# A hybrid decoder layer on one core: operands of the first gate/up row moved to VectorE, two weight loads and a statistic moved across a stage boundary

## The chip, the cores and the metric

The kernel runs on one core of a Trainium2 chip. A core has five engines with instruction queues of their own that run in the order written: TensorE (PE in the profile, its weight loads as PEld), VectorE (DVE), ScalarE (ACT), GpSimd (POOL) and SyncE (SP). They meet through semaphores. SP, ACT and POOL also issue DMAs. The metric is the device time of one execution in microseconds (us), as the median of three runs: 1428.53 us, from 1426.43 to 1428.83.

## The reference, cut to what matters

Batch 1, 1024 tokens, width 1024, all float32. Three sub-layers follow each other, each with a norm before and after:

```python
h = hybrid_mixer(rmsnorm(x, norms[l, 0]), ...)      # NSA attention (512) | short conv (512)
x = x + rmsnorm(h, norms[l, 1])
h = memory_attention(rmsnorm(x, norms[l, 2]), rmsnorm(mem, mem_norm[l]), mem_wq, mem_wkv, mem_wo)
x = x + rmsnorm(h, norms[l, 3])
h = swiglu(rmsnorm(x, norms[l, 4]), ffn_wg, ffn_wu, ffn_wd)   # hidden width 2816
x = x + rmsnorm(h, norms[l, 5])
# end of the mixer:
merged = jnp.concatenate([rmsnorm(o_nsa, gn_nsa), rmsnorm(o_conv, gn_conv)], axis=-1)
return merged @ w_out
# swiglu:
return (jax.nn.silu(h @ wg) * (h @ wu)) @ wd
```

## The kernel before, in words

Tokens are cut into eight rows of 128. A matmul operand is split into a high and a low part (`split`: ACT copies the high part at line 119, another engine subtracts for the low part at line 120), and a product is three matmuls, high by high, high by low and low by high (`mm3`, lines 123 to 125). With four blocks of depth a product is 12 matmuls of 512 columns.

The program has stages. **Attention** takes the token rows in order; for each pair of heads it leaves its output in the tile `on` (GpSimd, line 730), which SP stores to DRAM (`on_d`). After the last pair of a row the sum of squares of that row is made for the group norm: ScalarE squares `on` into `sq` (line 799), TensorE adds over partitions with `ones` (line 802), and `rsqrt` (VectorE, ScalarE twice, VectorE) leaves one column of `gn`. The projections of the conv half are filled in between. At its end GpSimd loads the output weights of the attention half (`load_wo`, line 199) and the query weights of the memory attention (`wq`, line 811, two tiles of 1 MB), and then the stage's other constants (line 848).

The **middle stage** holds the output projection, the memory attention and the norms. It is a list of small units in one line of text (`L` load, `M` split, `P` project, `N` norm, `X` transpose, `Q` query, ...). For token row n, `u_load` requests `on` (256 KB), `pt` (512 KB, the conv half) and `x` (512 KB) on SP; `u_merge` splits `on` into `mh` and `ml`; `u_proj` makes 24 matmuls `p<-big,mh`; `u_post` (lines 898 to 908) adds `pt`, normalises, adds to `x`. The tiles `on`, `pt` and `x` have two buffers each, and SP takes the requests in order. Sixteen products of the next stage (`G`, four for each of its rows 1 to 4) fill TensorE's time at the end.

The **gate/up stage** cuts tokens and depth in halves and multiplies 2 by 2 blocks with seven products instead of eight, for gate and for up. It runs over 11 rows j; a row takes the hidden columns of blocks j and j+11. A row needs the eight weight blocks `raw` (256 KB each, `ff_load`), sums and differences of these (`s3`, and in place in `raw`: lines 1184 to 1186 and 1190), splits of them (`ah`, `al`), and the token operands B11, B21, T2, T3, T1, T4, B22. In row 0 the latter five do not stand yet: `build_t` (line 1124) makes the differences of the token blocks and splits them. Row 0 has 14 products, rows 1 to 4 have 10 each. The **down stage** follows.

The order of instructions on each engine comes from a scheduler, which goes by priorities (the order of the code) and by its own estimate of when operands are there; DMAs may be bound to come after an instruction (`tc.issue_after`). So a change in one place moves instructions in others.

Of the kernel before, what the change touches and what calls it, by code (L numbers as in the profile page):

```python
# [66 lines left out]
def hymba_kernel(ctx: ExitStack, tc: tile.TileContext, a, out: bass.AP):  # L67
# [134 lines left out]
    with ExitStack() as st:  # L202
# [363 lines left out]
            load_wo(k)  # L566
        proj_k("s", C_KS)


    ap2 = pool(at_stack, "ap2", bufs=2)  # L570
    with ExitStack() as st:
# [120 lines left out]
        def pv_stage(i, h0, pc, psel, pwin, w0):  # L692
# [32 lines left out]
            if h0 % 4 == 2:  # L725
                tmp = ap2.tile([64, 2, 2, 2, P], F32, name="otmp", bufs=1)
                for x in range(2):
                    A.activation(tmp[:, x], po4[0][64 * x:64 * x + 64], AF.Copy)
                for par in range(2):
                    Gp.tensor_tensor(ons[i][par * 64:(par + 1) * 64, h0 // 2 - 1:h0 // 2 + 1, :],  # L730
                                     tmp[:, 0, :, par, :], tmp[:, 1, :, par, :], OP.add)
            if h0 == H - 2:
                Y.dma_start(on_d[i], ons[i])
# [48 lines left out]
        for n, (i, h0) in enumerate(tasks):  # L782
            ahead = run_soft(n + SKEW)
            pv = pv_stage(i, h0, cmps[i][1], *soft.pop(n))
            steps = next(pv)
            acc = OFF[i]
            for _ in pv:
                acc += RATE[i] / steps
                while acc >= 1:
                    acc -= 1  # L790
                    next(ahead, None)
            for _ in ahead:
                pass
            if n in (9, 21, 29, 30):
                with tc.issue_after(last["norm"].ins):
                    load_wo((9, 21, 29, 30).index(n))
            if h0 == H - 2:
                sq = ap2.tile([P, 4, P], F32, name="sq", bufs=1)
                A.activation(sq, ons[i], AF.Square)
                pn = psf.tile([P, 1], F32, name="f")  # L800
                for c in range(4):
                    T.matmul(pn, sq[:, c, :], ones[:, 0:1], start=c == 0, stop=c == 3)
                V.tensor_copy(gn[:, i:i + 1], rsqrt(small, pn, 512, 1, "gn"))
                for m in range(FILL[n // 4], FILL[n // 4 + 1]):
                    fill(m)
        for m in range(FILL[NT], 2 * NT):
# [1 line left out]
        wq = []  # L808
        for c in range(2):
            wq.append(big_tile().bitcast(F32R).rearrange("p a b -> p (a b)"))  # L810
            Gp.dma_start(wq[c], wq_d[c].rearrange("p x c -> p (x c)"))
            wq[c] = wq[c].rearrange("p (x k c) -> p x k c", x=2, k=KT)
    at_stack.close()

# [16 lines left out]
    def en(k):  # L831
        return V if EN[k] == "V" else Gp
# [39 lines left out]
    def u_merge(n):  # L872
        on = ld[n][0]
        mh = em.tile([P, 4, P], F32R, name="mh", bufs=2)
        ml = em.tile([P, 4, P], F32R, name="ml", bufs=2)
        split(mh, ml, on, en("M"))
        mrg[n] = mh, ml

    def u_proj(n):
        mh, ml = mrg.pop(n)  # L880
# [171 lines left out]
                fload(k)  # L1052

    def ff_raw():
        return ff["s"].tile([P, 4, P], F32, name="raw", bufs=10)

    def ff_load(w, q, j):
        c, k0 = (j + HF if q[0] == "2" else j), (4 if q[1] == "2" else 0)
# [59 lines left out]
    with ExitStack() as st:  # L1118
# [5 lines left out]
        def build_t():  # L1124
            hi = bp.tile([P, 4, 512], F32R, name="T2h")
            lo = bp.tile([P, 4, 512], F32R, name="T2l")
            for k in range(4):
                x0, x1, x2, x3 = a0[:, k, :], b0[:, k, :], a1[:, k, :], b1[:, k, :]
                V.tensor_tensor(x0, x1, x0, OP.subtract)
                tmp = sp1.tile([P, 512], F32, name="tmp")  # L1130
                V.tensor_tensor(tmp, x3, x0, OP.subtract)
                split(hi[:, k, :], lo[:, k, :], tmp, en("T2"))
                Gp.tensor_tensor(x1, x3, x1, OP.subtract)
                Gp.tensor_tensor(x2, x2, tmp, OP.subtract)
            bop["T2"] = hi, lo
            put_b("T3", b0, en("T3"), bp)
            put_b("T1", a0, en("T1"), bp)
            put_b("B22", b1, en("B22"), bp)
            put_b("T4", a1, en("T4"), bp)
# [3 lines left out]

        for j in range(HF):
            t = {}
            s1 = sp1.tile([P, S], F32, name="sg", bufs=3)
            s2 = sp1.tile([P, S], F32, name="sg", bufs=3)
            raw = {(w, q): ff_load(w, q, j) for w in range(2) for q in ("11", "12", "21", "22")}

            def put(w, dst, src0, src1):  # L1150
                if w == 0:
# [17 lines left out]
            for w in range(2):  # L1169
# [2 lines left out]
                    Y.dma_start(c, c1_d[j - 1, w])  # L1172
                    put(w, s1[:, ta], None, c)
                else:
                    put(w, s1[:, ta], prod(raw[w, "12"], "B21", Gp), t[w, 1])
            if j == 0:
                build_t()
                assert tc.cur_priority < after_mid + 3000, (tc.cur_priority, after_mid)
# [2 lines left out]
            for w in range(2):  # L1181
                s3 = late.tile([P, 4, P], F32, name="s3")
                t[w, "s3"] = s3
                Gp.tensor_tensor(s3, raw[w, "11"], raw[w, "21"], OP.subtract)  # L1184
                Gp.tensor_tensor(raw[w, "21"], raw[w, "21"], raw[w, "22"], OP.add)
                Gp.tensor_tensor(raw[w, "11"], raw[w, "21"], raw[w, "11"], OP.subtract)
            for w in range(2):
                m = prod(raw[w, "11"], "T2", V)
                V.tensor_tensor(t[w, 1], t[w, 1], m, OP.add)
                Gp.tensor_tensor(raw[w, "12"], raw[w, "12"], raw[w, "11"], OP.subtract)  # L1190
            for w in range(2):
                m = prod(t[w, "s3"], "T3", V)
                t[w, 3] = late.tile([P, 512], F32, name="t3")
# [230 lines left out]
```

## Time and profile before

| what | value |
|---|---|
| median of three runs | 1428.53 us |
| profiled execution, its own time | 1429.11 us |
| its span, from first to last instruction | 1427.3 us |
| mean granted TensorE clock | 0.974 |
| busy: PE / DVE / ACT / POOL | 1349.8 / 940.2 / 682.6 / 497.2 us |
| attention's last matmul of the main chain | about 567 us |
| middle stage's first projection | 579.85 us |
| gate/up row 0 on PE | 796.6 to 849.6 us |
| gate/up row 1 and later | 849.6 to about 1191 us |
| DMA | 203.28 MB, mean 142 GB/s |

The span is the time between the first and the last instruction; 1.8 us lie around it. A long busy share of PE does not say that PE is the limit everywhere: the profile's slices show two places where PE is idle and its clock is granted at half, near 570 us and near 810 us. There the question is which wait ends last. A "row" of a timeline gives the start, the time from the first start to the last end of the group, and in brackets how long the engine had been idle and what released it.

### The profile page before, as it was taken

The page shows a single profiled execution, that of the slowest core. Times are in us where ns is not written, and L with a number is a line of the kernel's source. Part 1 is how long each engine was busy: PE and PEld are TensorE (multiplying, and loading weights), DVE is VectorE, ACT ScalarE, POOL GpSimd, SP SyncE. Part 2 cuts the span into 40 slices and gives each one's busy share as a digit, 9 for nine tenths or more (in the row PEclk, how much of TensorE's full clock was granted, in tenths as well). Part 3 has the DMA queues.
Part 4 walks back from the last instruction along what each step waited for, and adds up shares of the span by engine and source line. Part 5 has one row for each costly group of instructions (what it writes and reads, how often), then busy time and mean ns, then how long its engine had stood idle before and what let it go on. Part 6 is the DMA issues. An engine that isn't in the chain of part 4 may idle for free.

```text
span 1427.3 us, 19754 instructions
## 1 busy us (share of the span) xinstructions
PE 1349.8 (95%) x6748; PEld 1127.1 (79%) x6748; DVE 940.2 (66%) x2071; ACT 682.6 (48%) x1465; POOL 497.2 (35%) x472
## 2 busy tenths in 40 slices
PE   8999999999999998798779899999999999989997
PEld 6987788888989887677668678888888887867885
DVE  6444553447899995468886786654544444998787
ACT  5433334327878886256675432333333333444463
POOL 1232332227767664111120766654444531000000
PEclk9999999999999999799989899999999999999999
DMA  7587466494733303943246455432222226930213
GB/s 229 146 282 266 142 221 194 151 233 104 149 67 68 75 8 133 351 158 104 91 136 195 125 170 158 144 118 74 89 89 82 82 89 214 375 112 30 67 59 118
DMA packets 161061, 203.28 MB, mean 142 GB/s; under 512 B 8530, under 2 KB 115198, under 8 KB 156703
## 3 DMA queue, kind: packets, MB, share of 16 engines
q1 hardware_dynamic: 128416, 146.44, 32.2%
q0 software_dynamic: 31392, 53.48, 13.5%
q10 hardware_dynamic: 1152, 2.10, 0.4%
q8 instruction: 53, 0.87, 0.3%
q14 instruction: 48, 0.39, 0.1%
HBM read 138.54 MB, written 63.44 MB: 142 GB/s over the span
## 4 chain that ended last, share of the span: by engine, by line
PE 75%; DVE 12%; issue 4%; DMA 4%; ACT 3%; POOL 1%; SPq 0%; DVEq 0%; POOLq 0%; ACTq 0%
PE m L125 13%; PE m L124 13%; PE m L123 13%; PE mm L125 4%; PE mm L123 4%; PE mm L124 4%; PE o L718 3%; PE t L712 2%; DVE ptl L120 1%; PE s L642 1%; PE s L643 1%; DVE psel L659 1%; PE mm L228 1%; PE tr L485 1%; PE p L123 1%
## 5 line engine op out<-in xcount | busy, mean ns | idle before, releaser
L119 ACT ACTIVATE ah<-raw 128x512 fp32r<-128x512 f32 x132 | 83.0, 631 | 212.3 <-PE m L124 188.8
L125 PE MATMUL mm<-hh,wl 128*128 128x512 f32 x320 | 125.5, 394 | 2.2 <-POOL wl L120 2.2
L123 PE MATMUL mm<-hh,wh 128*128 128x512 f32 x320 | 126.6, 396 | 0.1
L124 PE MATMUL mm<-hl,wh 128*128 128x512 f32 x320 | 125.6, 393 | 0.0
L120 DVE TENSOR_TENSOR al<-raw,ah 128x512 fp32r<-128x512 f32 x118 | 107.1, 908 | 24.8 <-ACT ah L119 24.8
L124 PE MATMUL m<-bl,ah 128*128 128x512 f32 x264 | 102.9, 397 | 3.7 <-DVE bl L120 3.7
L125 PE MATMUL m<-bh,al 128*128 128x512 f32 x264 | 102.0, 397 | 2.5 <-DVE al L120 2.5
L120 POOL TENSOR_TENSOR wl<-wr,wh 128x1024 fp32r<-128x1024 f32 x22 | 54.0, 2456 | 134.9 <-ACT wh L119 134.9
L1161 POOL TENSOR_TENSOR sg<-sg,tmp 128x512 f32<-128x512 f32 x44 | 66.0, 1500 | 80.6 <-DVE tmp L1160 36.8
L124 PE MATMUL m<-big,ah 128*128 128x512 f32 x232 | 92.3, 398 | 0.0
L120 DVE TENSOR_TENSOR ptl<-t,pth 128x512 fp32r<-128x512 f32 (+1 forms) x120 | 77.5, 657 | 16.1 <-ACT pth L119 16.0
L119 ACT ACTIVATE pth<-t 128x512 fp32r<-128x512 f32 (+1 forms) x120 | 66.8, 572 | 15.2 <-PE t L712 14.4
L125 PEld LDWEIGHTS mm<-hh,wl 128*128 128x128 f32 x320 | 60.8, 190 | 15.8 <-POOL wl L120 3.0
L123 PE MATMUL m<-bh,ah 128*128 128x512 f32 x264 | 71.8, 391 | 1.1 <-ACT bh L119 1.1
L123 PEld LDWEIGHTS mm<-hh,wh 128*128 128x128 f32 x320 | 60.9, 190 | 13.0 <-ACT wh L119 0.6
L124 PEld LDWEIGHTS mm<-hl,wh 128*128 128x128 f32 x320 | 60.9, 190 | 12.5
L124 PEld LDWEIGHTS m<-bl,ah 128*128 128x128 f32 x264 | 50.4, 191 | 15.9 <-DVE bl L120 5.3
L125 PEld LDWEIGHTS m<-bh,al 128*128 128x128 f32 x264 | 50.3, 192 | 14.4 <-DVE al L120 4.1
L1153 DVE TENSOR_TENSOR sg<-m,t 128x512 f32<-128x512 f32 x40 | 27.6, 690 | 49.0 <-PE m L125 42.2
L1160 DVE TENSOR_TENSOR tmp<-m,t 128x512 f32<-128x512 f32 x40 | 27.6, 691 | 48.6 <-PE m L125 22.1
L1184 POOL TENSOR_TENSOR s<-raw 128x512 f32<-128x512 f32 x22 | 29.7, 1352 | 85.9 <-DMA raw<-in_ffn_wu_dram 54.1
L123 PEld LDWEIGHTS m<-bh,ah 128*128 128x128 f32 x264 | 49.8, 189 | 12.1 <-ACT bh L119 1.6
(490 smaller groups left out, 4154.8 us busy)
## 6 DMA issues: line engine op xcount, KB each, us to landing
raw<-in_ffn_wg_dram SPq DMA_DIRECT2D x52, 256.0 KB, 3.1
raw<-in_ffn_wu_dram SPq DMA_DIRECT2D x52, 256.0 KB, 3.0
hid_d<-sg SPq DMA_DIRECT2D x22, 512.0 KB, 2.7
q<-in_ffn_wd_dram SPq DMA_DIRECT2D x44, 256.0 KB, 5.4
q<-hid_d SPq DMA_DIRECT2D x44, 256.0 KB, 5.4
wr<-in_w_in_dram SPq DMA_DIRECT2D x20, 512.0 KB, 4.4
x<-in_x_dram SPq DMA_DIRECT2D x16, 512.0 KB, 4.0
wo_d<-phl POOLq DMA_DIRECT2D x8, 1024.0 KB, 6.6
```

The lines of the kernel that those rows point to most:

```text
L119: A.activation(hi, src, AF.Copy)
L120: (lo_eng or V).tensor_tensor(lo, src, f(hi), OP.subtract)
L123: T.matmul(ps, lh, rh, start=start, stop=False)
L124: T.matmul(ps, lh, rl, start=False, stop=False)
L125: T.matmul(ps, ll, rh, start=False, stop=stop)
L228: T.matmul(ps, rbB[:, h, :], oh, start=True, stop=True)
L712: T.transpose(ps[:, m, j, :], pt[:, j, off * P:(off + 1) * P], ident)
L718: T.matmul(pof, vst[:, kt, b, g, :], t[:, m].rearrange("p h q -> p (h q)"), start=u + x + m == 0, stop=x == 1 and u + m == len(units) - 1)
L1153: V.tensor_tensor(dst, src0, src1, OP.add)
L1160: V.tensor_tensor(tmp, src0, src1, OP.add)
L1161: Gp.tensor_tensor(dst, dst, tmp, OP.mult)
L1184: Gp.tensor_tensor(s3, raw[w, "11"], raw[w, "21"], OP.subtract)
```

## The change

Five edits. (1) The statistic of the last token row (`group_stat`) is no longer made at the end of the attention but in the middle stage, in `u_merge` of that row, with a PSUM bank of that stage. (2) The two `wq` loads are bound to come after the last GpSimd addition into `on`. (3) In row 0 of gate/up the engine of the sums and differences, and of the low part of the B21 products, is VectorE (`ce`), and in `build_t` the two operations that GpSimd had are on VectorE as well, with a tile `t2` of three buffers. (4) The eight `raw` loads of each row go block by block, gate and up in turn, instead of four of gate and then four of up. (5) `raw` has 11 buffers instead of 10.

```diff
+    def group_stat(pl, pn, i, on):
+        sq = pl.tile([P, 4, P], F32, name="sq", bufs=1)
+        A.activation(sq, on, AF.Square)
+        for c in range(4):
+            T.matmul(pn, sq[:, c, :], ones[:, 0:1], start=c == 0, stop=c == 3)
+        V.tensor_copy(gn[:, i:i + 1], rsqrt(small, pn, 512, 1, "gn"))
...
-                    Gp.tensor_tensor(ons[i][par * 64:(par + 1) * 64, h0 // 2 - 1:h0 // 2 + 1, :],
+                    last["on"] = Gp.tensor_tensor(ons[i][par * 64:(par + 1) * 64, h0 // 2 - 1:h0 // 2 + 1, :],
...
             if h0 == H - 2:
-                sq = ap2.tile([P, 4, P], F32, name="sq", bufs=1)
-                A.activation(sq, ons[i], AF.Square)
...
+                if i != ORD[-1]:
+                    group_stat(ap2, psf.tile([P, 1], F32, name="f"), i, ons[i])
...
-            Gp.dma_start(wq[c], wq_d[c].rearrange("p x c -> p (x c)"))
+            with tc.issue_after(last["on"].ins):
+                Gp.dma_start(wq[c], wq_d[c].rearrange("p x c -> p (x c)"))
...
         mrg[n] = mh, ml
+        if ORD[n] == ORD[-1]:
+            group_stat(em, bank(U["X"], (P, 1)), ORD[n], on)
...
-        return ff["s"].tile([P, 4, P], F32, name="raw", bufs=10)
+        return ff["s"].tile([P, 4, P], F32, name="raw", bufs=11)
...
-                tmp = sp1.tile([P, 512], F32, name="tmp")
-                V.tensor_tensor(tmp, x3, x0, OP.subtract)
-                split(hi[:, k, :], lo[:, k, :], tmp, en("T2"))
-                Gp.tensor_tensor(x1, x3, x1, OP.subtract)
-                Gp.tensor_tensor(x2, x2, tmp, OP.subtract)
+                t2 = sp1.tile([P, 512], F32, name="t2", bufs=3)
+                V.tensor_tensor(t2, x3, x0, OP.subtract)
+                V.tensor_tensor(x2, x2, t2, OP.subtract)
+                split(hi[:, k, :], lo[:, k, :], t2, en("T2"))
+                V.tensor_tensor(x1, x3, x1, OP.subtract)
...
+            ce = Gp if j else V
-            raw = {(w, q): ff_load(w, q, j) for w in range(2) for q in ("11", "12", "21", "22")}
+            raw = {(w, q): ff_load(w, q, j) for q in ("11", "12", "21", "22") for w in range(2)}
...
-                    put(w, s1[:, ta], prod(raw[w, "12"], "B21", Gp), t[w, 1])
+                    put(w, s1[:, ta], prod(raw[w, "12"], "B21", ce), t[w, 1])
...
-                Gp.tensor_tensor(s3, raw[w, "11"], raw[w, "21"], OP.subtract)
-                Gp.tensor_tensor(raw[w, "21"], raw[w, "21"], raw[w, "22"], OP.add)
-                Gp.tensor_tensor(raw[w, "11"], raw[w, "21"], raw[w, "11"], OP.subtract)
+                ce.tensor_tensor(s3, raw[w, "11"], raw[w, "21"], OP.subtract)
+                ce.tensor_tensor(raw[w, "21"], raw[w, "21"], raw[w, "22"], OP.add)
+                ce.tensor_tensor(raw[w, "11"], raw[w, "21"], raw[w, "11"], OP.subtract)
...
-                Gp.tensor_tensor(raw[w, "12"], raw[w, "12"], raw[w, "11"], OP.subtract)
+                ce.tensor_tensor(raw[w, "12"], raw[w, "12"], raw[w, "11"], OP.subtract)
```

What the scheduler makes of it stands below. GpSimd's queue at the end of the attention, before (`big<-wq_d` are the query weights, `big<-wo_d` output weights, `on<-otmp` the last attention output):

```order
L199 DMA big<-wo_d_84 128x2048
L199 DMA big<-wo_d_85 128x2048
L811 DMA big<-wq_d_78 128x2048
L811 DMA big<-wq_d_79 128x2048
L730 TENSOR_TENSOR on<-otmp 64x256 x2
L848 DMA kmh<-km_d 128x1024
L848 DMA kml<-km_d 128x1024
```

And with the change:

```order
L199 DMA big<-wo_d_84 128x2048
L199 DMA big<-wo_d_85 128x2048
L738 TENSOR_TENSOR on<-otmp 64x256 x2
L816 DMA big<-wq_d_78 128x2048
L816 DMA big<-wq_d_79 128x2048
L853 DMA kmh<-km_d 128x1024
L853 DMA kml<-km_d 128x1024
```

The two `wq` requests now stand behind the last addition into `on`, and ahead of the same constants as before. ScalarE's queue at the same place, before (`mh<-on` is the first work of the middle stage):

```order
L728 ACTIVATE otmp<-o 64x512 x2
L799 ACTIVATE sq<-on 128x512
L108 ACTIVATE gny<-gnv 128x1
L109 ACTIVATE gny<-gny 128x1
L119 ACTIVATE mh<-on 128x512 x3
```

And with the change:

```order
L119 ACTIVATE pth<-t 128x256
L736 ACTIVATE otmp<-o 64x512 x2
L119 ACTIVATE mh<-on 128x512 x3
L896 ACTIVATE pt,ssq<-h 128x1024
L108 ACTIVATE rny<-rnv 128x1
```

Nothing stands any more between the last `otmp` and the first `mh`; the statistic's three activations come later in the queue, behind the splits of the token rows that the middle stage takes first. The middle stage's own units are interleaved anew on PE, DVE and ACT, with the same work in them.

VectorE's queue from the first operation of `build_t` to the split of row 0's first weight block, before (`T1l`, `T3l`, `big<-big,B22h` are low parts of token operands, `al` of weight blocks):

```order
L1129 TENSOR_TENSOR big<-big 128x512 x4
L120 TENSOR_TENSOR al<-raw,ah 128x512
L1089 TENSOR_TENSOR raw<-raw,s 128x512
L120 TENSOR_TENSOR T1l<-big,T1h 128x512 x3
L120 TENSOR_TENSOR T3l<-big,T3h 128x512
L120 TENSOR_TENSOR T1l<-big,T1h 128x512
L120 TENSOR_TENSOR T3l<-big,T3h 128x512 x3
L120 TENSOR_TENSOR big<-big,B22h 128x512 x4
L1089 TENSOR_TENSOR raw<-raw,s 128x512 x2
L120 TENSOR_TENSOR al<-raw,ah 128x512 x3
```

And with the change, in two pieces that follow each other (`t_8523` and the like are the four tiles `t2`):

```order
L1136 TENSOR_TENSOR big<-big 128x512 x4
L120 TENSOR_TENSOR al<-raw,ah 128x512
L1138 TENSOR_TENSOR t_8523<-big 128x512
L1141 TENSOR_TENSOR big<-big 128x512
L1096 TENSOR_TENSOR raw<-raw,s 128x512
L1138 TENSOR_TENSOR t_8530<-big 128x512
L1141 TENSOR_TENSOR big<-big 128x512
L120 TENSOR_TENSOR T1l<-big,T1h 128x512
L1138 TENSOR_TENSOR t_8537<-big 128x512
L1141 TENSOR_TENSOR big<-big 128x512 x2
L1139 TENSOR_TENSOR big<-big,t_8523 128x512
L120 TENSOR_TENSOR T1l<-big,T1h 128x512 x3
```

The second piece:

```order
L1139 TENSOR_TENSOR big<-big,t_8530 128x512
L120 TENSOR_TENSOR T2l<-t_8523,T2h 128x512
L120 TENSOR_TENSOR T3l<-big,T3h 128x512
L120 TENSOR_TENSOR T2l<-t_8530,T2h 128x512
L1139 TENSOR_TENSOR big<-big,t_8537 128x512
L120 TENSOR_TENSOR T3l<-big,T3h 128x512
L120 TENSOR_TENSOR T2l<-t_8537,T2h 128x512
L1096 TENSOR_TENSOR raw<-raw,s 128x512
L120 TENSOR_TENSOR T3l<-big,T3h 128x512 x2
L1096 TENSOR_TENSOR raw<-raw,s 128x512
L1138 TENSOR_TENSOR t_8544<-big 128x512
L120 TENSOR_TENSOR al<-raw,ah 128x512 x3
```

Ahead of the first `al` of row 0 stand 20 operations before and 30 now; ahead of the first `al` of a T2 product 53 now. TensorE's queue at the start of row 0, before (`m_8444`, `m_8463` are the B11 products of gate and up, `m_8481`, `m_8500` the B21 products):

```order
L123 MATMUL m_8444<-big_7724,ah_8445 128x512
L124 MATMUL m_8444<-big_7725,ah_8445 128x512
L125 MATMUL m_8444<-big_7724,al_8446 128x512
L123 MATMUL m_8444<-big_7724,ah_8445 128x512
L124 MATMUL m_8444<-big_7725,ah_8445 128x512
L125 MATMUL m_8444<-big_7724,al_8446 128x512
```

And with the change:

```order
L123 MATMUL m_8444<-big_7724,ah_8445 128x512
L124 MATMUL m_8444<-big_7725,ah_8445 128x512
L123 MATMUL m_8463<-big_7724,ah_8464 128x512
L124 MATMUL m_8463<-big_7725,ah_8464 128x512
L123 MATMUL m_8481<-B21h_7987,ah_8482 128x512
L124 MATMUL m_8481<-B21l_7988,ah_8482 128x512
L123 MATMUL m_8500<-B21h_7987,ah_8501 128x512
L124 MATMUL m_8500<-B21l_7988,ah_8501 128x512
L125 MATMUL m_8444<-big_7724,al_8446 128x512
```

Two matmuls of each of the four products, which need no low part of a weight block, now stand ahead of the first one that does; the ten left of each follow. In the same way two of each of the next five products (T2, T3 of gate and up, T1 of gate) stand ahead of the first `al` of T2, and then the ten left of each of these five and 12 of each of the last five products.

## Rows read from the trace of the kernel before

**Rows 1.** Windows: us, busy of each engine (count), clock, DMA share, GB/s.

```profile
560.00:580.00 20.00, 8.93 (x57) 8.01 (x55) 5.14 (x12) 6.59 (x13) 6.27 (x11) 0.77 0.94 351
...
680.00:700.00 20.00, 14.23 (x85) 11.20 (x84) 15.58 (x42) 16.71 (x52) 4.53 (x6) 1.00 0.28 104
```

**Rows 2.** Chain that ended last, 540 to 620: start us, us, what.

```profile
566.01 13.14 DMA on<-on_d
579.17 0.64 ACT mh L119
579.85 0.80 PE p L123
```

**Rows 3.** Timeline of ScalarE at the boundary: start, us, instruction, [idle before].

```profile
567.11 1.20 ACT L728 ACTIVATE otmp<-o 64x512 f32<-64x512 f32 x2 [1.13 <-PE o L718]
...
572.82 0.20 ACT L109 ACTIVATE gny<-gny 128x1 f32<-128x1 f32 x1
```

**Rows 4.** Timeline of GpSimd at the boundary.

```profile
560.67 1.24 POOL L199 DMA_DIRECT2D big<-wo_d  x2 [7.63 <-PE f L125]
562.06 0.53 POOL L811 DMA_DIRECT2D big<-wq_d  x1
...
568.39 1.49 POOL L730 TENSOR_TENSOR on<-otmp 64x256 f32<-64x256 f32 x2 [5.09 <-ACT otmp L728]
```

**Rows 5.** Line 199 (output weights), 500 to 640: time to landing.

```profile
DMA to landing us min/median/max: 5.3/6.3/7.4
```

**Rows 6.** Timeline of SP at the boundary.

```profile
563.69 0.45 SPq L865 DMA_DIRECT2D on<-on_d  x1
...
580.93 0.90 SPq L869 DMA_DIRECT2D x<-in_x_dram  x2
```

**Rows 7.** DMA queues, 568 to 574 us: packets, MB, share (q0 GpSimd, q1 SP).

```profile
q0 software_dynamic: 271, 1.96, 81.0%
q1 hardware_dynamic: 271, 0.53, 26.3%
```

**Rows 8.** DMA queues, 574 to 590 us.

```profile
q0 software_dynamic: 755, 3.83, 61.2%
q1 hardware_dynamic: 1020, 2.68, 45.7%
```

**Rows 9.** DMA queues, 590 to 595 us.

```profile
q1 hardware_dynamic: 599, 2.07, 102.3%
```

**Rows 10.** Timeline of VectorE: token row 0 is added to x.

```profile
596.21 0.69 DVE L902 TENSOR_TENSOR x<-x,h 128x512 f32<-128x512 f32 x1
```

**Rows 11.** Windows: row 0 of gate/up on PE, and a piece of it.

```profile
796.60:849.60 53.00, 45.18 (x170) 34.92 (x169) 39.83 (x46) 19.04 (x32) 36.95 (x25) 0.87 0.46 136
...
800.60:805.90 5.30, 5.28 (x12) 4.13 (x13) 1.46 (x1) 1.81 (x5) 5.22 (x5) 0.50 0.65 209
```

**Rows 12.** Windows: rows 1 to 10 of gate/up.

```profile
850.00:1190.00 340.00, 340.00 (x1466) 275.18 (x1465) 176.61 (x240) 106.02 (x171) 169.38 (x124) 1.00 0.33 103
```

**Rows 13.** Waits of PE, 780 to 1000: us in total, times, longest.

```profile
PE m L125 <- DVE al L120: 4.4, 2, 3.4
PE m L123 <- ACT T2h L119: 2.1, 1, 2.1
```

**Rows 14.** Timeline of VectorE around row 0.

```profile
783.92 4.71 DVE L1129 TENSOR_TENSOR big<-big 128x512 f32<-128x512 f32 x4 [1.75 <-ACT big L1029]
...
799.88 0.68 DVE L120 TENSOR_TENSOR al<-raw,ah 128x512 fp32r<-128x512 f32 x1
...
833.52 0.68 DVE L120 TENSOR_TENSOR big<-big,T4h 128x512 fp32r<-128x512 f32 x1
834.13 0.68 DVE L120 TENSOR_TENSOR al<-raw,ah 128x512 fp32r<-128x512 f32 x1
```

**Rows 15.** Timeline of GpSimd: its first work in `build_t`.

```profile
784.97 6.50 POOL L1133 TENSOR_TENSOR big<-big 128x512 f32<-128x512 f32 x4 [31.60 <-ACT big L1029]
```

**Rows 16.** Timeline of ScalarE: high parts of row 0's blocks.

```profile
800.13 1.67 ACT L119 ACTIVATE ah<-raw 128x512 fp32r<-128x512 f32 x3 [4.03 <-DMA raw<-in_ffn_wu_dram]
```

More of the change, by code (lines that the diff above doesn't have):

```diff
@@ L797, in hymba_kernel @@
             if h0 == H - 2:
-                sq = ap2.tile([P, 4, P], F32, name="sq", bufs=1)
-                A.activation(sq, ons[i], AF.Square)
[L800 to L803, printed above, removed]
+                if i != ORD[-1]:
+                    group_stat(ap2, psf.tile([P, 1], F32, name="f"), i, ons[i])
                 for m in range(FILL[n // 4], FILL[n // 4 + 1]):
```

## The prediction

> **What bounds the kernel now.** I began with the slices of the page, which show TensorE at full clock nearly everywhere except around 570 us and 810 us. From 850 to 1190 us PE is busy 340.00 of 340.00 us with 1466 matmuls, 0.232 us each [rows 12]: there PE is the limit, and a start that comes earlier by some microseconds ends earlier by as many. The other two places need the windows, the chain of waits and the queues.
>
> At the boundary between attention and middle stage PE works 8.93 of 20 us while the DMA engines are 0.94 busy [rows 1]. The chain goes through one transfer: SP requests `on` at 566.01, it lands 13.14 us later, ScalarE makes `mh` at 579.17, and the first projection starts at 579.85 [rows 2]. 256 KB in 13 us is a starved queue. From 568 to 574 us GpSimd's queue and SP's moved 271 packets each, but 1.96 MB against 0.53 MB [rows 7]: packet for packet, and GpSimd's are almost four times as large. SP thus got 0.53/6 = 0.088 MB/us; from 574 to 590 us it got 2.68/16 = 0.1675 MB/us [rows 8]; alone, it got 2.07/5 = 0.414 MB/us [rows 9]. What held the queue first is `wq`, requested from 562.06, before the last addition into `on` at 568.39 [rows 4].
>
> In row 0 of gate/up PE takes 53.00 us at a granted clock of 0.87 [rows 11]. Its 14 x 12 = 168 matmuls at 0.232 us would be 39. PE waits 4.4 us for `al` (3.4 in one piece) and 2.1 us for `T2h` [rows 13], and behind the long wait the clock is 0.50, the lower level of 1.2 GHz, for 5.3 us [rows 11].
>
> **Part by part: the boundary (edits 1 and 2).** ScalarE ends `otmp` at 567.11 + 1.20 = 568.31, and the old statistic holds it until 573.02 [rows 3]; so without edit 1 no `mh` could start before 573.0, wherever the loads stand, and without edit 2 `on` would be late still. With both, GpSimd's queue holds only output weights until they land, 560.67 + 7.4 = 568.1 [rows 4, 5], and `wq` goes out after 568.39 + 1.49 = 569.9 [rows 4]. The awaited `on` has one other `on` (requested at 563.69 [rows 6]) and one `pt` ahead of it: 0.26 + 0.52 + 0.26 = 1.05 MB, from 568.1 at 0.414 MB/us, lands at 570.6. With the 0.68 from the split's start to the first projection [rows 2] that starts at 571.3, 8.5 us earlier. If `wq` takes the engines at 569.9 at once, 0.3 MB are left at 0.088 and the gain is 5.9; if `on` is there when ScalarE comes free it is 579.17 - 568.31 = 10.9.
>
> Next late is `x`. SP requests it at 580.93, when the `on` buffers come free [rows 6]; that moves with the splits. On SP's queue it stands behind 3.9 MB in all (four `on`, one store, two `pt`, the norm weights, two `x`, at the sizes given above). 3.1 us alone move 1.28 MB until 571.2, then 6 us beside `wq` move 0.53, and the remaining 2.09 at 0.1675 need 12.5: it lands at 589.7. It is added at 596.21 now [rows 10], so wanted at 596.21 - 8.5 = 587.7. That is 2.0 us late (bounds 0, and 3.8 if beside `wq` nothing of it moves faster than 0.088 until 581), and 6.5 us are left.
>
> The statistic then costs the middle stage ScalarE time: one activation of the size of `mh`, 0.64 [rows 2], and two of 0.20 [rows 3], 1.0 us. That stage runs PE 14.23, VectorE 15.58 and ScalarE 16.71 of 20 us [rows 1]: nothing full, so half of it lies beside other work, and I take 0.5 (bounds 0 and 2, with VectorE's part). The units of the stage are also interleaved anew on three engines. No row prices an order. The idle share of the fullest engine, (20 - 16.71)/20 [rows 1], over the 217 us from 579.85 to 796.6 is 36 us, the most that an order could give or cost; the nearest is that the same units with the same operands take the same time, so 0, and I keep a tenth of it, 4, either way. **Place 1 gives 6.0 us.**
>
> The queue's share can be read against the Trainium skill, "DMA: Bandwidth & Descriptors", section "Issuing engines are not separate DMA queues": all issuers run on the same 16 DMA engines, so moving `wq` removes no bytes. The trace agrees, 9.0 MB in the 22 us of [rows 7, 8] being 0.41 MB/us, no more than SP alone had. That rule speaks against this edit; what it would do here is rival A.
>
> **Row 0 (edits 3 to 5).** Before, GpSimd does the four `x1` operations in 6.50 us beside VectorE, whose four take 4.71, 1.18 each [rows 14, 15]; the same form alone starts every 0.61 us (833.52 to 834.13) [rows 14]. After, GpSimd has no sum or difference left in row 0, so VectorE should keep 0.61. It has 30 operations ahead of the first `al`: 783.92 + 30 x 0.61 = 802.2, done 802.9, where it started at 799.88 before [rows 14]. PE starts row 0 at 796.6 as before; the eight leading matmuls last 1.9 us, then it waits 4.4 us instead of 3.4, and the half clock behind that stays. Then the weight blocks: 53 operations stand ahead of the first `al` of T2, 783.92 + 53 x 0.61 = 816.2, done 816.9. By then PE has finished the four first products and the ten leading matmuls. What is left, 5 x 10 + 5 x 12 = 110 matmuls, takes 25.5 us at 0.232: row 0 ends at 842.4 instead of 849.6, 7.2 us earlier. At 0.69 us an operation, a row's whole duration [rows 10], T2's `al` comes 4.2 later and the gain is 3.0; with the half clock gone too (5.3 x 0.5 = 2.6 [rows 11]) it is 9.8. I take 7.2, nearest to the pitch in the same stage.
>
> The order of the loads brings `wu`'s first block second instead of fifth: ScalarE's wait of 4.03 us for it before 800.13 [rows 16] ends, worth nothing by itself, since VectorE is later than that. The eleventh buffer serves later rows, in which PE has no gap [rows 12]: 0.
>
> **Sum.** 6.0 + 7.2 = 13.2. The profiled execution took 1429.11 us (span 1427.3 and 1.8 around it): 1415.9, and 0.6 less against the median, 1428.53: 1415.
>
> **Rivals.** A: the middle stage swallows the early start. The engines are full at the boundary [rows 1], and if SP gets only 2.62 MB in the 25 us from 571.2 to 596.21 (0.105 MB/us, between the 0.088 and 0.1675 of [rows 7, 8]), `x` lands no earlier than it is added now [rows 10]. Against it: once `wq`'s 2 MB have passed, 0.1675 is what the row shows. Then only row 0 gives: 1428.5 - 7.2 = 1421.
>
> B: VectorE's longer queue eats row 0's gain. With 23 operations between the first `al` and T2's `al`, and ScalarE's high parts between them, each wait for a high part adds to 816.2, and ScalarE itself waited 4.03 us there for a load [rows 16]. Row 0 gives 0 to 3: 1419.5 to 1422.5. Against it: ScalarE is busy 39.83 of 53 us only [rows 11].
>
> C, the slower side: VectorE becomes row 0's bound because GpSimd works beside it after all. At 1.18 us [rows 14] the 53 operations take 62.5 us, T2's `al` is done at 847.1, row 0 ends at 872.6, 23.0 later, and with place 1's 6.0 the kernel takes 1445.5. It decides from a pitch of (829.4 - 783.92)/53 = 0.86 us, where row 0 loses 6.0. For it: GpSimd's operands of row 1 (eight operations at 6.50/4 = 1.6 us [rows 15]) are made as soon as their blocks land, beside row 0's. Against it: all eight are 13 us, in which VectorE at 1.18 instead of 0.61 loses 13 x 0.57/1.18 = 6.3 us, less than the 13.2 between 816.2 and 829.4.
>
> The rule behind C stands in the Trainium skill, "SBUF — State Buffer", section "Who interferes with whom": VectorE's second port is shared with GpSimd under an exclusive lock. The trace agrees with it, 1.18 against 0.61 us; by it the edit removes the contention rather than brings it.
>
> D: both places fall through, or edits do not do what they say (`on` starved by the output weights, if they land later than in [rows 5]): within 0.2%, 1426 to 1431.
>
> **How the numbers follow.** Forecast 0.50, with a range of its own of 1409 to 1419 (the bounds of both places, 5.9 - 3.8 - 2 + 3 at the bad end, which already is A's, and 10.9 + 9.8 at the good, which needs all of them together). A 0.17, B 0.14, D 0.10, C 0.09. The range of 1408 to 1423 takes in the forecast, A and B, 0.81. A measurement here can tell 0.2%, some 2.9 us, from no change; faster by more than that are the forecast, A and B, 0.81; the same D, 0.10; slower C, 0.09.
>
> **What would show it.** In the changed profile: first projection at about 571.3, with `on` landing at 570.6; VectorE's add of `x` waiting about 2 us for a DMA; the last GpSimd additions ahead of `wq`. In row 0: length about 46 us, a PE wait of about 4 us for the first `al`, none for `T2h`, VectorE starts 0.61 us apart and GpSimd silent beside them; rows 1 to 10 without gaps. Wrong would be: a first projection after 575, a middle stage that ends when it did, or VectorE's operations above 0.86 us apart.

## The result, and the profile after

The changed kernel takes 1411.13 us (median of 5 runs, 1409.68 to 1414.08) where the kernel before takes 1427.35 (5 runs beside them): a ratio of 0.9887, 95% interval 0.9872 to 0.9902, 16.2 us faster. The forecast was 1415. In a later session the same kernel took 1409.44 beside 1427.32, ratio 0.9882 (0.9866 to 0.9898).

The profiled execution has a span of 1410.2 us, 17.1 less than before. Where the 17.1 lie is read from four points of the timelines (on ScalarE the end of the last `otmp`; on PE the first projection and the start of row 0 and of row 1 of gate/up):

| stretch | before, us | after, us | gained |
|---|---|---|---|
| start to the end of the last `otmp` | 568.31 | 566.87 | 1.44 |
| `otmp` to first projection | 11.54 | 4.48 | 7.06 |
| first projection to row 0 | 216.76 | 216.04 | 0.72 |
| row 0 | 52.97 | 46.01 | 6.96 |
| row 1 to the end | 577.72 | 576.80 | 0.92 |

The first line is not the change: the program is the same there, and its length differs between executions by some microseconds (the last `otmp` ended between 562.47 and 568.31 in the profiles of this study). The two places that the change aims at gave 7.06 and 6.96.

At the boundary the windows (columns as in [rows 1], the five busy times being those of PE, PEld, DVE, ACT and POOL) show PE busy 14.22 of 20 us where it was 8.93:

```profile
560.00:580.00 20.00, 14.22 (x69) 11.98 (x68) 3.77 (x6) 5.20 (x9) 5.60 (x10) 0.83 1.03 372
```

The timelines of GpSimd and of ScalarE answer to [rows 4] and [rows 3]. `wq` now goes out behind the additions, and ScalarE waits for `on` alone:

```profile
566.95 1.49 POOL L738 TENSOR_TENSOR on<-otmp 64x256 f32<-64x256 f32 x2 [6.47 <-ACT otmp L736]
568.38 1.10 POOL L816 DMA_DIRECT2D big<-wq_d  x2
```

```profile
565.67 1.20 ACT L736 ACTIVATE otmp<-o 64x512 f32<-64x512 f32 x2 [1.13 <-PE o L726]
568.68 0.63 ACT L119 ACTIVATE mh<-on 128x512 fp32r<-128x512 f32 x1 [1.81 <-DMA on<-on_d]
570.66 0.63 ACT L119 ACTIVATE mh<-on 128x512 fp32r<-128x512 f32 x1 [1.36 <-DMA on<-on_d]
```

The chain of waits has the same three links as [rows 2], the transfer at 6.08 us instead of 13.14:

```profile
564.57 6.08 DMA on<-on_d
570.66 0.64 ACT mh L119
571.35 0.80 PE p L123
```

The DMA queues from 568 to 572, 572 to 574 and 574 to 582 us show why: SP's queue had the engines nearly to itself until 572, 1.68 MB in 4 us, 0.42 MB/us, although `wq` was requested at 568.38.

```profile
q1 hardware_dynamic: 536, 1.68, 103.9%
...
q0 software_dynamic: 56, 0.46, 64.8%
q1 hardware_dynamic: 91, 0.22, 41.2%
...
q0 software_dynamic: 429, 2.38, 75.6%
q1 hardware_dynamic: 432, 0.87, 32.3%
```

GpSimd's packets begin 3.6 to 4.6 us after the request (the queues by single microseconds show its first ones, 0.16 MB, between 572 and 573). This is not what a GpSimd request takes as such: in the same trace the output weights were requested at 559.23, when no DMA ran, and their packets are there in the window from 560.4 to 560.6:

```profile
q0 software_dynamic: 6, 0.05, 228.5%
```

That is 1.3 us (the share means nothing in so short a window). Why `wq` took longer no run shows; what differs is that SP's queue was filling the engines. With that lead `x` is there in time: VectorE adds it at 588.19 straight behind the norm, with no wait in the brackets.

In row 0 VectorE keeps a steady pitch. Its timeline (the rows that answer to [rows 14]) has the first operations of `build_t`, the first `al`, and the first `al` of T2:

```profile
774.64 2.50 DVE L1136 TENSOR_TENSOR big<-big 128x512 f32<-128x512 f32 x4 [1.12 <-ACT big L1036]
...
792.69 1.89 DVE L120 TENSOR_TENSOR al<-raw,ah 128x512 fp32r<-128x512 f32 x3
...
806.54 0.68 DVE L120 TENSOR_TENSOR al<-raw,ah 128x512 fp32r<-128x512 f32 x1
```

(792.69 - 774.64)/30 = 0.602 and (806.54 - 774.64)/53 = 0.602 us an operation. PE's waits from 780 to 1000 us answer to [rows 13]; the windows are row 0, the piece of it at half clock (1.2 GHz), and rows 1 to 10. The last fence is from the kernel before, a second piece of its row 0 at half clock, which [rows 11] don't show:

```profile
PE m L123 <- ACT ah L119: 3.6, 3, 1.7
PE m L123 <- DVE raw L1096: 1.3, 1, 1.3
```

```profile
787.39:833.40 46.01, 41.86 (x169) 31.86 (x170) 41.14 (x58) 17.41 (x28) 18.81 (x12) 0.96 0.56 170
791.98:795.40 3.42, 3.09 (x7) 2.08 (x8) 3.42 (x7) 0.63 (x1) 0.00 (x0) 0.50 0.93 285
834.00:1174.00 340.00, 340.00 (x1466) 275.21 (x1465) 174.36 (x239) 104.92 (x170) 165.79 (x122) 1.00 0.31 98
```

```profile
816.49:823.31 6.82, 5.86 (x15) 4.07 (x14) 6.72 (x7) 1.26 (x2) 4.97 (x4) 0.50 0.27 75
```

The waits for `al` and for `T2h` of [rows 13] are gone; 4.9 us of others stand in their place, of which 0.7 lie ahead of row 0's first matmul and 4.2 in the row. The clock is a good half of the gain. Row 0 had two pieces at half clock, the one of [rows 11], in which PE was busy 5.3 us, and the one above, busy 5.9; now it has one, busy 3.1. At half clock PE starts a matmul every 0.43 us (794.02 to 794.45) where it is 0.23 at full clock, so by an estimate from these rows the clock gives about (5.3 + 5.9 - 3.1)/2 = 4 us and the shorter waits the rest. Rows 1 to 10 are gap-free as before, so all that row 0 gives is kept.

### The profile page after: what moved, and what is told of

It reads as the page before. It is cut to its first block, busy times and chain, and to the rows that moved or that the text cites. A ratio compares the mean times of both kernels' runs of the same rounds, so it can differ in the third digit from the quotient of the medians.

```text
span 1410.2 us, 19760 instructions
## 1 busy us (share of the span) xinstructions
PE 1344.6 (95%) x6748; PEld 1125.7 (80%) x6748; DVE 939.1 (67%) x2089; ACT 683.1 (48%) x1465; POOL 468.1 (33%) x454
## 4 chain that ended last, share of the span: by engine, by line
PE 76%; DVE 13%; ACT 3%; issue 3%; DMA 2%; POOL 1%; SPq 0%; DVEq 0%; POOLq 0%; ACTq 0%
PE m L125 13%; PE m L124 13%; PE m L123 13%; PE mm L123 5%; PE mm L125 5%; PE mm L124 4%; PE o L726 3%; PE t L720 2%; DVE ptl L120 1%; PE s L650 1%; DVE psel L667 1%; PE s L651 1%; PE mm L228 1%; PE tr L485 1%; PE o L124 1%
## 5 line engine op out<-in xcount | busy, mean ns | idle before, releaser
L120 DVE TENSOR_TENSOR al<-raw,ah 128x512 fp32r<-128x512 f32 x120 | 107.6, 899 | 17.2 <-ACT ah L119 17.1
L119 ACT ACTIVATE ah<-q 128x512 fp32r<-128x512 f32 (+2 forms) x55 | 30.0, 545 | 60.5 <-PE m L124 58.6
```

Of the source, the lines that this page charges most:

```text
L119: A.activation(hi, src, AF.Copy)
L120: (lo_eng or V).tensor_tensor(lo, src, f(hi), OP.subtract)
```

## The experiments

Times beside "before" are those of the kernel before on the same chip in the same session; the stage lengths are read as in the table above. In sum:

| run | median / before, us | ratio, 95% interval | `otmp` to first projection | middle | row 0 |
|---|---|---|---|---|---|
| edit 2 alone | 1421.85 / 1426.45 | 0.9966 (0.9951, 0.9981) | 4.49 | 216.31 | 57.93 |
| edit 1 alone | 1433.24 / 1426.45 | 1.0041 (1.0025, 1.0058) | 11.51 | 219.48 | 57.88 |
| edit 3 alone | 1422.60 / 1426.45 | 0.9970 (0.9957, 0.9983) | 11.73 | 219.30 | 46.59 |
| edits 4, 5 alone | 1423.80 / 1426.45 | 0.9974 (0.9961, 0.9988) | 11.56 | 216.35 | 49.13 |
| edits 3 to 5 | 1420.25 / 1427.32 | 0.9958 (0.9942, 0.9973) | 11.79 | 218.93 | 46.60 |
| all but edit 1 | 1411.11 / 1426.17 | 0.9885 (0.9867, 0.9903) | 4.50 | 217.21 | 46.12 |
| all but edit 4 | 1409.43 / 1426.17 | 0.9877 (0.9861, 0.9892) | 4.41 | 213.86 | 45.99 |
| GpSimd busy beside | 1430.93 / 1426.17 | 1.0035 (1.0024, 1.0047) | 4.54 | 232.63 | 50.30 |
| row 0 reordered | 1407.28 / 1426.17 | 0.9860 (0.9843, 0.9877) | 4.51 | 214.80 | 44.79 |
| that, token row 0 first | 1416.67 / 1427.32 | 0.9932 (0.9916, 0.9947) | 2.48 | 226.22 | 44.79 |

The middle stage lasted 216.76 in the kernel before and 219.30 with edit 3 alone, whose PE order there is the same. The difference arises between 659 and 710 us, ahead of every instruction that edit 3 moves, so 3 us of this stage are no evidence.

**Edit 2 alone.**

```diff
-                    Gp.tensor_tensor(ons[i][par * 64:(par + 1) * 64, h0 // 2 - 1:h0 // 2 + 1, :],
+                    last["on"] = Gp.tensor_tensor(ons[i][par * 64:(par + 1) * 64, h0 // 2 - 1:h0 // 2 + 1, :],
...
-            Gp.dma_start(wq[c], wq_d[c].rearrange("p x c -> p (x c)"))
+            with tc.issue_after(last["on"].ins):
+                Gp.dma_start(wq[c], wq_d[c].rearrange("p x c -> p (x c)"))
```

> Edit 2 alone: wq requested after the last addition into on, statistic still at the end of the attention. My prediction's step (ScalarE is held by the statistic for 4.7 us after otmp, so the first split cannot start before that ends) expects the first projection about 2.5 to 3 us later than with both edits, measured from the end of the last otmp: 571.35 - 566.87 = 4.5 us with both, 12.4 without, so about 7 here, and a kernel 4 to 6 us faster than before (1421 to 1423). Rival: the scheduler now puts mh between the squares and the two small activations, so only the squares (0.63 us, behind GpSimd's addition) stand ahead of mh: about 5 us after otmp, a kernel some 7 us faster (1420), and edit 1 is worth nothing or under 1 us.

The rival holds at the boundary. ScalarE's timeline:

```profile
564.72 1.20 ACT L728 ACTIVATE otmp<-o 64x512 f32<-64x512 f32 x2 [1.13 <-PE o L718]
567.52 0.63 ACT L799 ACTIVATE sq<-on 128x512 f32<-128x512 f32 x1 [1.61 <-POOL on L730]
568.06 0.61 ACT L119 ACTIVATE mh<-on 128x512 fp32r<-128x512 f32 x1
569.73 0.63 ACT L119 ACTIVATE mh<-on 128x512 fp32r<-128x512 f32 x1 [1.06 <-DMA on<-on_d]
570.30 0.20 ACT L108 ACTIVATE gny<-gnv 128x1 f32<-128x1 f32 x1
```

With `on` expected earlier, the scheduler put both `mh` between the squares and the small activations; the squares fit into the time in which `on` was still on its way. The kernel gained only 4.6 us of the boundary's 7, since row 0 took 57.93 us instead of 52.97. PE's waits there:

```profile
PE m L125 <- DVE al L120: 4.1, 2, 3.4
PE m L124 <- DVE T2l L120: 3.8, 2, 2.9
PE m L123 <- ACT T2h L119: 2.5, 2, 2.1
```

In the kernel before, the wait for T2l is shorter:

```profile
PE m L124 <- DVE T2l L120: 1.3, 1, 1.3
```

The two T2 products, whose operands come one by one off GpSimd's chain, are interleaved differently on PE: before, six T1 matmuls stand between pieces of them, and all of T3 ahead; here 22 T2 matmuls stand together, with three of T3 still behind them, and wait for T2l. The waits are 10.4 us in all instead of 7.8, and the mean clock of row 0 is 0.85 instead of 0.87. The same instructions in another order cost 5 us.

**Edit 1 alone.** `wq` stays where it was.

```diff
-                sq = ap2.tile([P, 4, P], F32, name="sq", bufs=1)
...
+                if i != ORD[-1]:
+                    group_stat(ap2, psf.tile([P, 1], F32, name="f"), i, ons[i])
...
+        if ORD[n] == ORD[-1]:
+            group_stat(em, bank(U["X"], (P, 1)), ORD[n], on)
```

> Edit 1 alone: the statistic moved to the middle stage, wq still requested ahead of the last addition. Theory (the transfer of on is what ends the wait, and wq's packets starve it): the first projection still comes about 12 us after otmp, kernel 0 to 1 us from before (1426.5 to 1428.5). Rival (ScalarE's statistic is the wait): 3 us or more faster.

The theory on the transfer holds, 13.11 us for `on` as before:

```profile
563.40 13.11 DMA on<-on_d
576.53 0.64 ACT mh L119
577.22 0.80 PE p L123
```

That the kernel became 6.8 us slower was expected by neither: row 0 has the same length and waits as in the run before (57.88 us, T2l 3.6), with the 22 T2 matmuls together on PE as there; and the middle stage is 2.7 longer, which cannot be told from what it varies.

**Edit 3 alone.** The new `build_t` of the change, and `ce` at its five places, of which one stands here:

```diff
+            ce = Gp if j else V
...
-                Gp.tensor_tensor(s3, raw[w, "11"], raw[w, "21"], OP.subtract)
+                ce.tensor_tensor(s3, raw[w, "11"], raw[w, "21"], OP.subtract)
```

> Edit 3 alone: all of row 0's sums and differences and the two operations of build_t on VectorE; loads in the old order, 10 buffers, boundary as before. Theory (the move to VectorE is what shortens row 0, by taking the contention and GpSimd's slow chain out): VectorE starts 0.61 us apart, row 0 lasts 46 to 48 us instead of 53.0, kernel 5 to 7 us faster (1420 to 1422). Rival (the order of the loads was needed too, since the up blocks come fifth): row 0 50 to 53 us, kernel 0 to 3 us faster.

Row 0 as the theory says, 46.59 us. The median gained less, 3.9 us; the profile has the 6.4 of row 0 and the middle stage 2.5 longer. How much of the row's gain is the contention and how much GpSimd's slow chain, this run doesn't separate, since the edit takes out both.

**Edits 4 and 5 alone.**

```diff
-        return ff["s"].tile([P, 4, P], F32, name="raw", bufs=10)
+        return ff["s"].tile([P, 4, P], F32, name="raw", bufs=11)
...
-            raw = {(w, q): ff_load(w, q, j) for w in range(2) for q in ("11", "12", "21", "22")}
+            raw = {(w, q): ff_load(w, q, j) for q in ("11", "12", "21", "22") for w in range(2)}
```

> Edits 4 and 5 alone: gate and up blocks requested in turn, 11 buffers; sums on GpSimd, boundary as before. Theory (worth nothing by itself since VectorE comes later than the loads): row 0 still 52 to 53 us, kernel within 1 us of before. Rival (ScalarE's 4.03 us wait for the load of up is part of PE's stall): PE's first stall shrinks by up to 3 us, the half clock behind it too, kernel 3 to 5 us faster.

The theory fails: row 0 is 49.13 us, 3.8 shorter, and the kernel 2.7 us faster. But the rival's mechanism isn't seen either, which was a first stall shorter by up to 3 us. PE's waits in row 0:

```profile
PE m L123 <- ACT T2h L119: 4.1, 1, 4.1
PE m L125 <- DVE al L120: 2.9, 1, 2.9
...
PE m L124 <- DVE T2l L120: 0.2, 1, 0.2
```

The waits alone don't give it: the first stall shrank from 3.4 to 2.9 and a second one of 1.0 for `al` went [rows 13], that for T2l shrank from 1.3 to 0.2, while that for T2h grew from 2.1 to 4.1: 7.2 us instead of 7.8. Their places changed, and with them the clock: in the windows row 0 has a mean clock of 0.93 where [rows 11] have 0.87, 0.06 of 50 us, 3 us.

```profile
793.49:842.62 49.13, 41.86 (x170) 32.95 (x168) 40.36 (x47) 19.64 (x33) 38.00 (x25) 0.93 0.53 156
```

PE's order in row 0 also moved a little (two T3 matmuls now stand among the T2 ones), so the landing of the blocks and the order on PE aren't separated here. Edit 5 was never run by itself.

**Edits 3 to 5.** The two diffs above together.

> Edits 3 to 5 without 1 and 2: row 0 as in the changed kernel, boundary as before. If the two places add up, the gain here is the row's 7 us and the boundary's 7 us are missing: row 0 46 us, first projection 11.5 us after otmp, about 1419 where the kernel before takes 1426. Rival (the places lean on each other, as the run with edit 2 alone suggests, whose row 0 was 5 us longer in another order on PE): row 0 stays at 46 us here, since its order on PE no longer changes with the boundary, and what edit 2 lost alone is the whole of the interaction.

Row 0 46.60 us, 7.1 us faster than before. Edit 2 alone gave 4.6; together 11.7, all edits 16.2 and 17.9 in two sessions. The 4.5 to 6.2 that the sum lacks agree with the 5.0 that edit 2 alone lost in row 0: with the operands on VectorE, row 0 takes 46.0 to 46.6 us with the old boundary and with the new one. So the rival holds.

**All but edit 1.** Against the changed kernel:

```diff
-                if i != ORD[-1]:
-                    group_stat(ap2, psf.tile([P, 1], F32, name="f"), i, ons[i])
+                sq = ap2.tile([P, 4, P], F32, name="sq", bufs=1)
+                A.activation(sq, ons[i], AF.Square)
...
-        if ORD[n] == ORD[-1]:
-            group_stat(em, bank(U["X"], (P, 1)), ORD[n], on)
```

> The changed kernel without edit 1: the last row's statistic stays at the end of the attention, edits 2 to 5 as they are. By my prediction's step edit 1 is needed for the boundary: the first projection about 2.5 us later and the kernel some 2 to 3 us slower than the changed one (1411.1), about 1413.5. Rival, after the run with edit 2 alone (first projection 4.49 us after otmp, as with both): edit 1 is worth nothing, 1410 to 1412, ratio to before 0.988 to 0.990, and row 0 again 46 us.

1411.11, 4.50 us to the first projection: the rival holds, and edit 1 is worth nothing that could be measured here (the interval of its ratio is 2.6 us to either side).

**All but edit 4.** Against the changed kernel:

```diff
-            raw = {(w, q): ff_load(w, q, j) for q in ("11", "12", "21", "22") for w in range(2)}
+            raw = {(w, q): ff_load(w, q, j) for w in range(2) for q in ("11", "12", "21", "22")}
```

> The changed kernel without edit 4: the four gate blocks requested first, then the four up blocks; all else as changed. Loads alone had given 3.8 us of row 0 beside GpSimd's sums. Theory A (with the sums on VectorE, VectorE's 53 operations set row 0, the loads are early enough): row 0 46 to 47 us, 1410 to 1412.5. Theory B (the order of the loads is a part of the gain here as well): row 0 48 to 50 us, 1413 to 1415.

Theory A: row 0 is 45.99 us. Edits 4 and 5 give 3.8 us of row 0 beside GpSimd's sums, and the order of the loads gives nothing once VectorE's list sets the row.

**GpSimd busy beside VectorE.** The result of the 20 subtractions is not used.

```diff
+            if j == 0:
+                jk = sp1.tile([P, S], F32, name="sg", bufs=3)
+                for q in range(20):
+                    Gp.tensor_tensor(jk[:, q % 2 * 512:q % 2 * 512 + 512], b1[:, 0, :], b1[:, 1, :], OP.subtract)
```

> The changed kernel with 20 useless GpSimd subtractions of 128x512 (two SBUF inputs) put beside VectorE's list at the start of row 0; their result is not used. It makes rival C on purpose. Theory (contention of 1.18 us for each of VectorE's operations while GpSimd works): GpSimd needs about 20 x 1.6 = 32 us or a little more, VectorE loses 32 x 0.57/1.18 = 15 us until T2's first al, which then comes at about 822 instead of 806.5 on the changed kernel's clock; row 0 60 us instead of 46.0, kernel 1425. Rival (GpSimd beside VectorE costs VectorE little, and the gain of row 0 came from GpSimd's slow chain alone): row 0 46 to 49 us, kernel 1411 to 1414.

It is the theory, with a price larger than it had. VectorE's and GpSimd's timelines:

```profile
781.55 0.67 DVE L1096 TENSOR_TENSOR raw<-raw,s 128x512 f32<-128x512 f32 x1
782.15 1.16 DVE L1138 TENSOR_TENSOR t<-big 128x512 f32<-128x512 f32 x1
...
803.40 1.75 DVE L120 TENSOR_TENSOR T2l<-t,T2h 128x512 fp32r<-128x512 f32 x1
805.07 1.75 DVE L1139 TENSOR_TENSOR big<-big,t 128x512 f32<-128x512 f32 x1
806.74 0.68 DVE L120 TENSOR_TENSOR T3l<-big,T3h 128x512 fp32r<-128x512 f32 x1
```

```profile
772.92 33.35 POOL L1157 TENSOR_TENSOR sg<-big 128x512 f32<-128x512 f32 x20 [32.76 <-ACT big L1036]
```

While GpSimd works, 33.35/20 = 1.67 us an operation, VectorE starts one every 1.67 us too (803.40 to 805.07): they take turns, one for one. When GpSimd ends at 806.3, the pitch is 0.6 at once. T2's first `al` starts 52.9 us after the first operation of `build_t` (824.79 and 771.87) instead of 31.9: VectorE lost 21 us where 15 were expected. Line 1096, one of whose two inputs lies in PSUM, takes 0.67 in the midst of it. The Trainium skill, "SBUF — State Buffer", section "Who interferes with whom", says just that of VectorE instructions with two SBUF inputs against those with one; this trace agrees. The wait fell ahead of row 0 (PE stood 11.7 us for its first `ah`), so middle stage and row 0 are to be taken together: 282.9 us against 262.1, 20.9 longer, and the kernel 4.8 slower than before.

**Row 0 reordered.**

```diff
-            put_b("T3", b0, en("T3"), bp)
+            with tc.issue_after(last["l4"].ins):
+                put_b("T3", b0, en("T3"), bp)
             put_b("T1", a0, en("T1"), bp)
-            put_b("B22", b1, en("B22"), bp)
-            put_b("T4", a1, en("T4"), bp)
...
+            if j == 0:
+                with tc.issue_after(last["s12"].ins), tc.issue_after(last["a4"].ins):
+                    put_b("T4", a1, en("T4"), bp)
             for w in range(2):
                 put(w, s2[:, ta], prod(raw[w, "22"], "T4", V), t[w, 3])
+            if j == 0:
+                with tc.issue_after(last["s12"].ins), tc.issue_after(last["a4"].ins):
+                    put_b("B22", b1, en("B22"), bp)
```

`l4` and `a4` are row 0's fourth `al` and `ah`, `s12` the last sum of its weight blocks.

> The changed kernel with row 0's lists in another order: T4 and B22 are split only after the sums of the weight blocks, T3 after the four first al, and ScalarE's copies of T4 and B22 after the four first ah. Same instructions, no work left out. In the changed kernel VectorE has 30 operations ahead of the first al and 53 ahead of T2's; here about 26 and 46. Theory (VectorE's list sets row 0): T2's al 7 x 0.6 = 4 us earlier, PE's waits of 4.9 us in row 0 shrink to 1 to 2, row 0 42 to 43.5 us, kernel 1407 to 1409. Rival (ScalarE or the loads take over as the wait): row 0 45 to 46 us, kernel 1410.5 to 1411.5.

1407.28 (1404.64 to 1408.58), against 1411.11 (1409.40 to 1413.65) of the run without edit 1, which is as fast as the changed kernel, on the same chip; with four runs each, the intervals of the two ratios overlap. T2's `al` is done earlier as expected: VectorE starts it at 801.11, 27.7 us after `build_t` instead of 31.9. But row 0 is 44.79 us, not 42 to 43.5. PE's waits in it:

```profile
PE m L123 <- DVE raw L1096: 1.3, 1, 1.3
PE m L125 <- DVE al L120: 1.0, 1, 1.0
PE m L123 <- ACT ah L119: 0.9, 2, 0.5
```

4.2 us of waits in the row became 3.2, and the row is 1.2 us shorter, not 2.5 to 4: T2's `al` was not what PE waited for (see below), and the wait for line 1096 to free its bank stayed. The rest of the gain against the changed kernel lies in the middle stage (214.80) and cannot be told from its variation. Its median is the lowest of the study, though not clear of the run without edit 4 (1409.43).

**The same, token row 0 first.** In the list of units, of which only the first four change places:

```diff
-    run("L1 L0 M1 M0 P0 P1 C0 L2
+    run("L0 L1 M0 M1 P0 P1 C0 L2
```

> The reordered row 0 of the run e8, and in the middle stage token row 0 loaded and split ahead of token row 1 (the first projection needs row 0's, which stood second in SP's queue behind 0.78 MB). Theory: on of token row 0 lands about 2 us earlier (568.7 instead of 570.7 on the changed kernel's clock), the first projection 2.5 us after otmp instead of 4.5, kernel 1.5 to 2 us faster than e8's 1407.3, about 1405.5. Rival (the next transfers, pt and x, are late then, or the middle stage's chain takes it up): no change, 1407.

The first projection does come 2.48 us after `otmp`, and by the two ratios (0.9932 against 0.9860) the kernel is 0.7% or 10 us slower than without this edit. The middle stage takes 226.22 us. PE's waits from 565 to 790 us name what is new, a wait of 6.3 us for the query side (2.6 in the run without it):

```profile
PE o L123 <- DVE qm L935: 6.3, 1, 6.3
```

Behind the earlier start the rest of the stage stands in another order on PE. That has the outcome of rival A, on another edit: the stage swallows the early start, and more. Whether the new order or the earlier start is to blame, no run separates.

**The changed kernel again.**

> The changed kernel itself once more, on the chip of these runs, as the measure for the others: about 1411, ratio to before 0.988 to 0.990, row 0 46.0 us, first projection 4.5 us after otmp.

1409.44, first projection 4.22 us after `otmp`, row 0 46.05 us: as before.

## Why the prediction was right, point by point

- *The transfer of `on` bounds the boundary, and `wq` starves it.* Shown: edit 1 alone leaves the transfer at 13.11 us and the first projection 11.51 behind `otmp`, edit 2 alone brings it to 4.49. The landing at 570.6 was measured at 570.65, but that is luck: `otmp` came 1.44 earlier in that execution, and relative to it the gain is 7.06, not 8.5. Two terms were too short. The 7.4 of [rows 5] belong to the second request, which was made at 561.4 and so landed at 568.8, not at 568.1 (before and, second line, with the change, where it was 559.9 + 7.8 = 567.7):

```profile
DMA to landing us min/median/max: 7.4/7.4/7.4
...
DMA to landing us min/median/max: 5.4/6.6/7.8
```

And `on` landed 2.9 us behind them, not 2.5. That `wq`'s packets stay out of the way until `on` has landed the sum took without a row (its bound of 5.9 is the other case); the late start of GpSimd's packets made it true.
- *"Without edit 1 no `mh` could start before 573.0."* This step failed. I took the order on ScalarE as given; it moved when edit 2 moved `on`, as an order that follows the scheduler's own estimate of when `on` arrives would. The run with edit 2 alone starts `mh` at 568.06 and 569.73, and edit 1 is worth nothing.
- *`x` is late next, by 2.0 us.* It was not: the estimate let `wq`'s packets run from 571.2 at once against SP, and left SP 1.28 MB until then; SP had 1.68 MB from 568 to 572 alone. The statistic's 0.5 and the reordering's 0 cannot be told from the 3 us by which the middle stage varies.
- *Row 0 gives 7.2.* Measured 6.96, and T2's first `al` where 53 operations of 0.60 us put it. But the waits were others. At the row's start PE waited 2.9 us for `ah` and the bank of line 1096, not 4.4 for `al`. Nor did it wait for T2's `al`, on which the sum rests: that was done at 807.22, and PE came to it at 807.73, behind its ten leading matmuls. What held it there was T2's first `ah`:

```profile
804.92 0.50 PE L123 MATMUL m<-T2h,ah 128*128 128x512 f32 x1 [1.21 <-ACT ah L119]
```

ScalarE makes it from a sum of the weight blocks (line 1194, VectorE at 803.53), which stands five operations ahead of that `al` in the same list. So VectorE's list does decide, through its sums. The second piece at half clock isn't in the prediction's account of the row before; its sum counts matmuls at full clock behind T2's `al`, and so contains that gain without naming it.
- *The loads' order is worth nothing.* Right in this change (all but edit 4: 45.99 us), wrong as said, "by itself": with edit 5 beside it, it gives 3.8 us of row 0.
- *Rival B.* Its counterargument misread [rows 11]: the 39.83 us are VectorE's, and ScalarE was busy 19.04. The right number speaks against B more strongly, and B did not come.
- *Rival C.* The mechanism is real and the change stays clear of it, GpSimd having nothing beside VectorE until 809. Its price was too low: 1.67 us an operation, not the 1.18, which is a mean over the four of [rows 14], the first of them started before GpSimd ([rows 15]: 784.97).
- *The whole.* 13.2 was forecast in the profile's terms and 17.1 came: boundary 1.4 less, `x` and the statistic 3.2 more (2.5 of cost that did not come, 0.7 gained), row 0 0.2 less, and 2.4 in stretches that the change doesn't touch, which are luck.

## What to carry to other kernels

A load that nobody needs soon, with packets larger than its neighbours', belongs behind the small transfer that the next stage waits for; judge it by what the other queue moved meanwhile, not by its own share. Where a scheduler orders the queues, an edit's effect isn't additive: the same edit was worth 7 us at its place and cost 5 us elsewhere, until another edit had taken GpSimd's chain out of that place. And when two engines with two SBUF inputs each are put side by side, the faster one runs at the slower one's pitch, so work off the slow engine can pay although the fast one is the busier.

## What the runs showed of the hardware that was not expected

In the run with GpSimd busy, VectorE and GpSimd alternate in operations of 128x512 with two inputs in SBUF (1.67 us against 0.60 alone), and an operation with one input in PSUM passes between (0.67). While SP's queue filled the engines at 0.42 MB/us, GpSimd's request of 568.38 moved its first bytes after 572; with no DMA running, one moved them after 1.3 us.
